# A convolution's taps move from a shared SBUF sum to PSUM, and a key/value product becomes a split product

## Chip, cores and metric

One core of one Trainium2 chip (8 cores, of which the program uses core 0). The metric is device time in microseconds (us) of one execution, the median of a few runs. Engines: TensorE (PE; PEld is its weight load), VectorE (DVE), ScalarE (ACT), GpSimd (POOL), SyncE (SP, which issues the DMAs here).

## What is computed

The program is a four-layer stack over 512 positions of width 1024, in fp32. Two hybrid layers (retention, dilated attention, gating, feed-forward) come first, then two layers of a second block. The second block's last layer begins with the convolution module, which the change is about, followed by cross attention to a memory of 256 positions and a gated feed-forward:

```python
def conv_module(xn, w_in, b_in, dw_w, dw_b, ln_g, ln_b, w_out):
    h = xn @ w_in + b_in
    a, gate = jnp.split(h, 2, axis=-1)
    h = a * jax.nn.sigmoid(gate)
    h = lax.conv_general_dilated(          # depthwise, causal, 31 taps
        h, dw_w[:, None, :], window_strides=(1,), padding=[(CONV_WIDTH - 1, 0)],
        dimension_numbers=('NWC', 'WIO', 'NWC'), feature_group_count=D_CONV) + dw_b
    h = jax.nn.silu(layernorm(h, ln_g, ln_b))
    return h @ w_out

def cross_attn(hn, memn, wq, wk, wv, q_gain, k_gain, wo):
    ...
    k = rmsnorm((memn @ wk).reshape(bsz, m_len, C_HEADS, C_HEAD_DIM), k_gain)
    v = (memn @ wv).reshape(bsz, m_len, C_HEADS, C_HEAD_DIM)
    ...
```

## The kernel before

**Products.** Nearly every matrix product is a split product: each fp32 operand is held as a high part (fp32r) and the low rest, and `mm3` (L325 to L328) issues three matmuls, high x high, high x low, low x high. Weights arrive by DMA from SP into `raw`; ScalarE casts the high part (L239) and VectorE, or GpSimd where `W.low` says so, subtracts it for the low part (L240), into one of eight slots `hl`. A few products are plain fp32 matmuls on the raw weights (L437) with no split; the keys and values of the last layer's memory are among them (`PLAIN_KV`).

**Order.** The order of instructions on each engine is fixed when the program is built. A modelled clock `X` runs a list of steps (a duration and a function that issues instructions); `X.at` puts a function at a modelled time, `X.drain` issues what is still due. Weights come in the order of `_weight_tiles`. An engine executes its instructions in that order, and waits at the head of its queue.

**The convolution** (`conv`) keeps channels on partitions: eight groups g of 128 channels by 512 positions. `prod` makes group g's two halves, value and gate, in two PSUM banks; `evac` (L1446 to L1448) turns them into `hp[:, g]`, with 30 zero columns ahead, by a tanh and an identity on ScalarE and one scalar-tensor-tensor on VectorE. Then 31 taps per group have to be summed into `y[:, g]` (SBUF):

- Groups 0 to 5: 18 taps on VectorE and 13 on GpSimd (`NPOOL`). A VectorE tap is one instruction, `y = hp * w + y` (L1520), with `w` a per-partition scalar. A GpSimd tap is a ScalarE product `m = hp * w` (L1510, three buffers) and a GpSimd add `y = y + m` (L1511). Both engines sum into the same `y[:, g]`, one after the other: in half of the groups GpSimd has the first phase, in the others VectorE.
- Groups 6 and 7: 14 taps on TensorE, as matmuls with diagonal weight matrices (L1559; VectorE makes the diagonals, L1552), copied by ScalarE to `y` (L1566), and 17 taps on VectorE (L1562), those of group 7 by halves of the sequence, with the second half put off (`late`).

A planner (`feed`, `choose`, `tap`) hands out taps from one queue per engine while PE steps run, by modelled costs (`T_TAP`, `T_SPLIT`, `T_SAME`: a tap that follows a tap into the same sum is counted 0.12 us dearer).

**The memory.** While this goes on, the layer's memory is normalised (L993), transposed and multiplied by the key and value weights in 16 steps of `memory_kv`, of four plain matmuls each: 10 of them before the means (`KV_LN`), 2 inside the first normalisation, and 4 inside the output product.

**After the taps.** The layer norm over channels is done per half of the sequence, 256 positions each: means by a ones matmul on PE (L1582), `spread` (L1611 on VectorE, a square on ScalarE, L1612), `total` (L1619, small variance matmuls), a reciprocal root and `across` (L1629), then per group `scale` (L1633 on VectorE, silu and cast on ScalarE, L1634 and L1635) and `apply` (low part). The output product takes four blocks t of 128 positions, each over eight weight tiles k and two banks; t 0 and 1 need the first half of the sequence, t 2 and 3 the second. The normalisation of the second half is put 14 modelled us (`AT_B`) after the first, so that it falls behind block 1, and the four remaining key/value steps stand ahead of block 2 (`before`). Six of the output weight tiles are held ahead (`AHEAD`), split in turn by GpSimd and VectorE (`LOW`).

## Time and profile before

| | |
|---|---|
| median of 3 runs | 2893.55 us (2886.67 to 2895.28) |
| profiled execution | 2889.6 us, span 2887.8 us, mean granted PE clock 0.983 |
| PE | 2758.8 us busy, 96% |
| PEld | 2289.5 us, 79% |
| DVE | 1341.2 us, 46% |
| ACT | 995.6 us, 34% |
| POOL | 484.3 us, 17% |

The profile is of one execution. Busy shares are averages over the whole span; the convolution, from about 2.09 to 2.39 ms, is a stage of its own in which they are different. Where a view speaks of a tap, the names are `y<-hp,conv_w,y`: the output, then the inputs (`conv_w` is the tile behind the pointer scalar `w`). `b` is any PSUM bank. Ends of matmuls are modelled, and fp32 matmuls have two records for one matmul of the program, so that counts on the rows of L437, L1559, L1582 and L1619 stand for half as many.

### The profile page before, as it was taken

Reading aid. Unit: us, or ns where it says so; the run is one execution under the profiler, and the core shown is the slowest. Engines: PE = TensorE matmul, PEld = TensorE weight load, DVE = VectorE, ACT = ScalarE, POOL = GpSimd, SP = SyncE. Lnnn points to the kernel's source line nnn. Section 1 sums busy time; section 2 is a strip of 40 time slices with the busy share of each in tenths; the row PEclk is TensorE's granted clock in tenths of the full one; section 3 lists DMA queues with packets and bytes.
Section 4 is the critical chain, followed back from the end, with each engine's and each line's share of the span. In section 5 each row is a group of like instructions: output and inputs, shape, how many; then the busy total and the mean of one; then the engine's idle time right before and its main releaser. Section 6 shows DMA issues by size and latency. Waiting matters only on the chain.

```text
span 2887.8 us, 34096 instructions
## 1 busy us (share of the span) xinstructions
PE 2758.8 (96%) x13624; PEld 2289.5 (79%) x13624; DVE 1341.2 (46%) x1952; ACT 995.6 (34%) x1737; POOL 484.3 (17%) x480
## 2 busy tenths in 40 slices
PE   7999999999999999999999999999995799999999
PEld 7888888879788888887678888888873368888887
DVE  4565222444464223355965442233499944432232
ACT  3434222333434223244454432223353235322231
POOL 3231000022130000023441300000076503100000
PEclk9999999999999999999999999999997899999999
DMA  4222322323213223222232213233231113132231
GB/s 149 76 72 76 114 95 88 124 62 103 69 60 102 96 94 117 91 78 81 78 116 74 94 54 107 90 105 114 83 106 51 66 44 103 52 103 97 93 117 51
DMA packets 76192, 255.95 MB, mean 89 GB/s; under 512 B 10369, under 2 KB 11777, under 8 KB 76033
## 3 DMA queue, kind: packets, MB, share of 16 engines
q1 hardware_dynamic: 76032, 253.77, 26.8%
q8 instruction: 107, 1.75, 0.2%
q14 instruction: 53, 0.43, 0.0%
HBM read 251.64 MB, written 2.10 MB: 88 GB/s over the span
## 4 chain that ended last, share of the span: by engine, by line
PE 82%; DVE 11%; ACT 3%; POOL 2%; issue 2%; DMA 0%; POOLq 0%; ACTq 0%; SPq 0%; DVEq 0%
PE b L326 25%; PE b L327 25%; PE b L328 25%; DVE y L1520 3%; PE b L348 1%; DVE y L1562 1%; DVE hl L240 1%; PE b L1402 1%; PE b L437 1%; DVE mask L1180 1%; ACT hl L239 1%; PE b L723 1%; DVE mask L1185 0%; POOL y L1511 0%; PE b L758 0%
## 5 line engine op out<-in xcount | busy, mean ns | idle before, releaser
L326 PE MATMUL b<-xh,hl 128*128 128x512 f32 (+1 forms) x1728 | 641.4, 371 | 1.6 <-ACT xh L336 1.6
L327 PE MATMUL b<-xl,hl 128*128 128x512 f32 (+1 forms) x1728 | 639.9, 370 | 1.7 <-DVE xl L337 1.7
L328 PE MATMUL b<-xh,hl 128*128 128x512 f32 (+1 forms) x1728 | 639.3, 370 | 0.0
L240 DVE TENSOR_TENSOR hl<-raw,hl 128x1024 fp32r<-128x1024 f32 (+1 forms) x398 | 471.8, 1210 | 149.6 <-ACT hl L239 146.2
L239 ACT CAST hl<-raw 128x1024 fp32r<-128x1024 f32 (+1 forms) x452 | 448.1, 1014 | 101.8 <-PE b L328 64.3
L326 PE MATMUL b<-hl,xh 128*128 128x512 f32 (+2 forms) x1088 | 412.8, 379 | 3.8 <-ACT xh L1635 1.7
L328 PE MATMUL b<-hl,xl 128*128 128x512 f32 (+2 forms) x1088 | 399.4, 367 | 3.2 <-DVE xl L337 3.0
L327 PE MATMUL b<-hl,xh 128*128 128x512 f32 (+2 forms) x1088 | 399.0, 367 | 2.5 <-DVE hl L240 2.4
L517 DVE TENSOR_TENSOR hraw<-sg,b 128x512 f32<-128x512 f32 (+1 forms) x96 | 61.8, 643 | 675.2 <-PE b L328 664.0
L326 PEld LDWEIGHTS b<-xh,hl 128*128 128x128 f32 x1728 | 326.4, 189 | 58.3 <-ACT xh L336 2.8
L327 PEld LDWEIGHTS b<-xl,hl 128*128 128x128 f32 x1728 | 326.4, 189 | 57.4 <-DVE xl L337 2.7
L328 PEld LDWEIGHTS b<-xh,hl 128*128 128x128 f32 x1728 | 326.2, 189 | 55.2
L516 ACT ACTIVATE sg<-b 128x512 f32<-128x512 f32 (+1 forms) x96 | 54.1, 563 | 675.2 <-PE b L328 675.2
L326 PE MATMUL b<-hl,hh 128*128 128x512 f32 x704 | 274.4, 390 | 0.0
L328 PE MATMUL b<-hl,hlw 128*128 128x512 f32 x704 | 273.9, 389 | 0.0
L327 PE MATMUL b<-hl,hh 128*128 128x512 f32 x704 | 273.9, 389 | 0.0
L326 PEld LDWEIGHTS b<-hl,xh 128*128 128x128 f32 x1088 | 208.2, 191 | 30.9 <-issue 5.7
L328 PEld LDWEIGHTS b<-hl,xl 128*128 128x128 f32 x1088 | 207.5, 191 | 27.2 <-DVE xl L337 4.4
L327 PEld LDWEIGHTS b<-hl,xh 128*128 128x128 f32 x1088 | 208.3, 191 | 23.4 <-DVE hl L240 3.7
L337 DVE TENSOR_TENSOR hlw<-hraw,hh 128x512 fp32r<-128x512 f32 x88 | 60.5, 691 | 210.5 <-ACT hh L336 210.5
L328 PEld LDWEIGHTS b<-hl,hlw 128*128 128x128 f32 x704 | 132.1, 188 | 27.5
L327 PEld LDWEIGHTS b<-hl,hh 128*128 128x128 f32 x704 | 132.2, 188 | 27.2
(276 smaller groups left out, 3132.5 us busy)
## 6 DMA issues: line engine op xcount, KB each, us to landing
raw<-in_ws SPq DMA_DIRECT2D x400, 512.0 KB, 3.5
raw<-in_ws SPq DMA_DIRECT2D x64, 384.0 KB, 3.1
x<-in_x SPq DMA_DIRECT2D x4, 512.0 KB, 6.4
mem<-in_mem SPq DMA_DIRECT2D x4, 512.0 KB, 5.4
out<-x SPq DMA_DIRECT2D x4, 512.0 KB, 2.6
raw<-in_ws SPq DMA_DIRECT2D x4, 336.0 KB, 2.8
gain<-in_g_mix_pre SPq DMA_DIRECT2D x2, 512.0 KB, 5.7
gain<-in_g_mix_post SPq DMA_DIRECT2D x2, 512.0 KB, 4.6
```

Of the source, the lines that this page charges most:

```text
L239: self.nc.scalar.copy(t[:, 0, :w], r[:, :w])
L240: self.low.tensor_sub(t[:, 1, :w], r[:, :w], t[:, 0, :w].bitcast(F32))
L326: PE.matmul(o, lh, rh, start=first, stop=False)
L327: PE.matmul(o, lh, rl, start=False, stop=False)
L328: PE.matmul(o, ll, rh, start=False, stop=last)
L337: (low or V).tensor_sub(dl, src, dh.bitcast(F32))
L348: PE.transpose(b[:, kk * P:(kk + 1) * P], xn[:, k * P:(k + 1) * P], ident)
L437: PE.matmul(b[:, :n], src[0][:, k, cols(t)], wh[:, kk], start=k == 0, stop=k == KD - 1)
L516: S.activation(sg[:, c0:c1], gb[:, c0:c1], AF.Silu)
L517: V.tensor_mul(hraw[:, n, c0:c1], sg[:, c0:c1], ub[:, c0:c1])
L723: PE.matmul(s[hh][:, :n], qkT["aq"][rs, pr, cols(t)], qkT["ak"][rs, pr, :n], start=True, stop=True)
L1520: V.scalar_tensor_tensor(o, i, w, o, op0=OP.mult, op1=OP.add)
```

## The change

VectorE no longer sums into `y`. Each group gets a PSUM bank `acc[g]`; VectorE's taps read `hp` and the bank and write the bank (`dve_tap`), GpSimd's sum stays in `y` (SBUF) and holds the bias, and one VectorE instruction per group adds the bank to `y` (`join`). For groups 6 and 7 the 14 diagonal matmuls start the sum in the same bank. GpSimd has 11 taps of 31 in groups 0 to 5 and now 6 in groups 6 and 7; VectorE has 20 and 11. With two sums no phase follows another, and the group products use banks 0 to 3 instead of 0 to 5, since banks 4 to 7 hold sums. ScalarE makes the diagonal matrices, 28 activations of 128 x 128, where VectorE made eight instructions.

The last layer's memory is split like everything else: its 16 weight tiles are cast and subtracted, and each key/value step is 12 matmuls instead of 4. 13 steps stand before the means, with group 7's diagonals ahead of the 13th, 3 stand inside the first half's normalisation, none in the output product. Weight order: the key/value tiles, then the output's, and none held ahead. The late half of group 7 goes; the second half's normalisation is issued right behind the first.

```diff
-PLAIN_KV = (1,)
-NPOOL = (13,) * 6
+NPOOL = (11,) * 6 + (6, 6)
-KV_LN = 10
-KV_OUT = 12
-AT_B = 14.0
-AT_PE = (1, 5)
-T_TAP = (0.72, 1.35)
+KV_LN = 13
+AT_PE = 12
+T_TAP = (0.78, 1.35)
...
-        out = by_rows(a["conv_w_out_2"][0]) if l else iter(())
-        for _ in range(AHEAD if l else 0):
-            yield next(out)
-        for i, w in enumerate((wk[:, :512], wk[:, 512:], wv[:, :512], wv[:, 512:])):
-            for t in moving(w):
-                yield t, l in PLAIN_KV
-                yield from itertools.islice(out, 1)
+        for w in (wk[:, :512], wk[:, 512:], wv[:, :512], wv[:, 512:]):
+            yield from moving(w)
+        if l:
+            yield from by_rows(a["conv_w_out_2"][0])
...
-            if l in PLAIN_KV:
-                mem["h"], mem["l"] = pl.tile([P, KD, 256], F32, tag="iq", name="mem"), None
+            if l:
+                mem["h"], mem["l"] = xh[:, :, 256:512], xl[:, :, 256:512]
...
+        where = {g: 4 + g % 2 for g in range(KD - 2)} | {KD - 2: 7, KD - 1: 6}
...
+        def pool_tap(g, j, first):
+            if first:
+                G.tensor_scalar(y[:, g, :], hp[:, g, j:j + T], dw[:, g, j:j + 1], db[:, g:g + 1], op0=OP.mult, op1=OP.add)
+            else:
+                m = pl.tile([P, T], F32, tag="m", name="m", bufs=4)
+                S.activation(m, hp[:, g, j:j + T], AF.Copy, scale=dw[:, g, j:j + 1])
+                G.tensor_add(y[:, g, :], y[:, g, :], m)
+
+        def dve_tap(g, j, first):
+            i, w = hp[:, g, j:j + T], dw[:, g, j:j + 1]
+            if first:
+                acc[g] = bank(where[g])
+                V.tensor_scalar(acc[g], i, w, None, op0=OP.mult)
+            else:
+                V.scalar_tensor_tensor(acc[g], i, w, acc[g], op0=OP.mult, op1=OP.add)
+
+        def join(g):
+            V.tensor_add(y[:, g, :], y[:, g, :], acc.pop(g))
+            joined.add(g)
+            ready.extend(((0, g), (1, g)))
...
-            def dve_tap(j, first, last):
-                o, i, w = y[:, g, :], hp[:, g, j:j + T], dw[:, g, j:j + 1]
...
-                    V.scalar_tensor_tensor(o, i, w, o, op0=OP.mult, op1=OP.add)
...
         def diagonals(g):
             st["dg", g] = d = []
-            for i, tag in enumerate(("s", "s", "s", "th")):
-                d.append(pl.tile([P, 4, P], F32, tag=tag, name="dg", bufs=3 if tag == "s" else 1))
-                V.tensor_tensor(d[i], ident[:, None, :].to_broadcast([P, 4, P]),
-                                dw[:, g, 4 * i:4 * i + 4, None].to_broadcast([P, 4, P]), op=OP.mult)
+            for i in range((NPE + 3) // 4):
+                d.append(pl.tile([P, 4, P], F32, tag="dg", name="dg", bufs=4))
+                for j in range(4 * i, min(4 * i + 4, NPE)):
+                    S.activation(d[i][:, j - 4 * i], ident, AF.Copy, scale=dw[:, g, j:j + 1])
...
-                        st[g] = [bank(2 * (g % 3)), bank(2 * (g % 3) + 1)]
+                        st[g] = [bank(2 * (g % 2)), bank(2 * (g % 2) + 1)]
...
-        X.drain()
+        means()
         means(True)
-        norm_half(0, 0.0, kv_steps[KV_LN:KV_OUT])
+        W.low = G
+        norm_half(0, 0.45, kv_steps[KV_LN:])
         X.drain()
         W.low = V
-        rest(1000)
-        X.at(AT_B, lambda: means(True))
-        X.at(AT_B, lambda: norm_half(1, 0.0))
+        norm_half(1, 0.55)
...
-            if t == 2 and k == 0:
-                X.run(kv_steps[KV_OUT:])
```

**How the order moves.** In the rows below, `b_` and a number is one PSUM bank in one use, and a count behind a row means the same instruction again. VectorE, the end of the taps in front of the means before:

```order
L1520 SCALAR_TENSOR_TENSOR y<-hp,conv_w,y 128x512 x20
L240 TENSOR_TENSOR hl<-raw,hl 128x1024
L1520 SCALAR_TENSOR_TENSOR y<-hp,conv_w,y 128x512 x4
L1562 SCALAR_TENSOR_TENSOR y<-hp,conv_w,y 128x512 x9
L1014 SCALAR_TENSOR_TENSOR kn<-b_16281,sm,g_15643 128x256 x2
L1014 SCALAR_TENSOR_TENSOR kn<-b_16282,sm,g_15643 128x256 x2
L1552 TENSOR_TENSOR dg<-ident,conv_w 128x512 x4
L1562 SCALAR_TENSOR_TENSOR y<-hp,conv_w,y 128x512 x5
```

and of the change (`b_16524`, `b_16310` and `b_16737` are the sums of three groups; L1588 is the subtraction of the mean, L1611 before):

```order
L229 TENSOR_TENSOR hl<-raw,hl 128x1024 x3
L1511 SCALAR_TENSOR_TENSOR b_16524<-hp,conv_w,b_16524 128x512 x3
L1514 TENSOR_TENSOR y<-y,b_16524 128x512
L1511 SCALAR_TENSOR_TENSOR b_16310<-hp,conv_w,b_16310 128x512 x8
L1514 TENSOR_TENSOR y<-y,b_16310 128x512
L1511 SCALAR_TENSOR_TENSOR b_16737<-hp,conv_w,b_16737 128x512 x11
L1514 TENSOR_TENSOR y<-y,b_16737 128x512
L1588 TENSOR_TENSOR y<-y,b_16823 128x256 x8
```

The taps read and write a bank, a join ends each group, weight splits (L240, now L229) stand among the taps up to the end, and the diagonals are gone from VectorE.

PE, from the first half's normalisation into the output product (L326 to L328, after it L315 to L317, are one split product). Before, where the product starts, and where the second half's normalisation stands (a row block t later):

```order
L1629 MATMUL b_16719<-ident,sm 128x128 x2
L326 MATMUL b_16775<-hl,xh 128x512
L327 MATMUL b_16775<-hl,xh 128x512
L328 MATMUL b_16775<-hl,xl 128x512
...
L328 MATMUL b_16829<-hl,xl 128x512
L1582 MATMUL b_16304<-y,ones 128x256
L1619 MATMUL b_16849<-ones,s 128x2 x16
L1629 MATMUL b_16895<-ident,sm 128x128 x2
L326 MATMUL b_16828<-hl,xh 128x512
```

and of the change:

```order
L1596 MATMUL b_16841<-ones,s 128x2 x8
L1606 MATMUL b_16923<-ident,sm 128x128 x2
L315 MATMUL b_16992<-hl,xh 128x512
L316 MATMUL b_16992<-hl,xh 128x512
L317 MATMUL b_16992<-hl,xl 128x512
L315 MATMUL b_16993<-hl,xh 128x512
L316 MATMUL b_16993<-hl,xh 128x512
L317 MATMUL b_16993<-hl,xl 128x512
L1596 MATMUL b_16988<-ones,s 128x2 x2
L315 MATMUL b_16992<-hl,xh 128x512
```

The second half's variance matmuls (`b_16988`) stand behind the first six matmuls of the output product, in pairs between its following blocks, and no longer all together behind one of its row blocks.

ScalarE at the same place (L1634 and L1635 are the silu and the cast of `scale`, L1612 the squares of the second half, L1030 a copy of values). Before:

```order
L1634 ACTIVATE s<-y,conv_ln_b,conv_ln_g 128x256
L1635 CAST xh<-s 128x256
L1030 COPY vt<-b_16613 128x512
L1030 COPY vt<-b_16614 128x512
L1612 ACTIVATE s<-y 128x256 x8
```

and of the change (L1611, L1612 and L1589 are the silu, the cast and the squares; L228 the cast of a weight; five more silu and cast pairs stand where the dots are):

```order
L1611 ACTIVATE s<-y,conv_ln_b,conv_ln_g 128x256
L1612 CAST xh<-s 128x256
L228 CAST hl<-raw 128x1024 x2
L1611 ACTIVATE s<-y,conv_ln_b,conv_ln_g 128x256
L1612 CAST xh<-s 128x256
L228 CAST hl<-raw 128x1024
...
L1611 ACTIVATE s<-y,conv_ln_b,conv_ln_g 128x256
L1612 CAST xh<-s 128x256
L228 CAST hl<-raw 128x1024
L1589 ACTIVATE s<-y 128x256 x8
```

The weight casts of the output product now stand among the first half's silu and cast pairs, and the squares of the second half behind all of them.

## Rows read from the trace of the kernel before

**Rows 1.** The page, the span in 40 equal slices of 72.2 us: tenths of VectorE's busy time, and the granted clock of PE in tenths.

```profile
DVE  4565222444464223355965442233499944432232
PEclk9999999999999999999999999999997899999999
```

**Rows 2.** Windows of the convolution: its taps up to the last tap of the first half, and a stretch inside it. Columns: the window, its length, busy us (and instructions) of PE, PEld, DVE, ACT and POOL, granted clock, DMA share, GB/s.

```profile
2097.80:2302.90 205.10, 154.54 (x508) 97.76 (x506) 199.10 (x182) 83.77 (x137) 144.54 (x91) 0.87 0.22 74
2196.00:2219.00 23.00, 6.11 (x11) 2.62 (x10) 22.96 (x15) 10.45 (x15) 22.14 (x14) 0.65 0.14 51
```

**Rows 3.** The chain of waits from the last tap to the output product's first matmul, and at its end the first matmul of the next stage: start and length in us, engine, output, line.

```profile
2303.01 0.71 PE b L1582 x2
...
2306.34 5.06 PE b L437 x8
...
2313.53 3.54 PE b L437 x8
...
2319.00 0.50 PE b L326
...
2389.84 0.47 PE b L326
```

**Rows 4.** Groups of VectorE instructions between 2085 and 2360 us, kept apart by shape: line, engine, operation, out<-in, sizes, count | busy us, mean ns of one | idle us just before them and what ended most of it.

```profile
L1520 DVE SCALAR_TENSOR_TENSOR y<-hp,conv_w,y 128x512 f32<-128x512 f32 x105 | 122.6, 1209 | 2.1 <-POOL y L1511 1.2
L1562 DVE SCALAR_TENSOR_TENSOR y<-hp,conv_w,y 128x512 f32<-128x512 f32 x17 | 24.7, 1455 | 0.4
L1562 DVE SCALAR_TENSOR_TENSOR y<-hp,conv_w,y 128x256 f32<-128x256 f32 x34 | 16.4, 482 | 0.7
L1448 DVE SCALAR_TENSOR_TENSOR hp<-th,av 128x512 f32<-128x512 f32 x6 | 7.4, 1226 | 0.0
L993 DVE SCALAR_TENSOR_TENSOR mem<-mem,sm,gain 128x1024 f32<-128x1024 f32 x2 | 4.5, 2309 | 0.0
L1014 DVE SCALAR_TENSOR_TENSOR kn<-b,sm,g 128x256 f32<-128x256 f32 x8 | 3.3, 476 | 0.0
```

**Rows 5.** Timeline of VectorE and GpSimd inside the taps: start and length in us of a run of like instructions, engine, line, count, and in brackets the idle time ahead of it. The first two stretches have no GpSimd instruction beside them; the last two lie beside each other.

```profile
2098.38 2.33 DVE L1520 SCALAR_TENSOR_TENSOR y<-hp,conv_w,y 128x512 f32<-128x512 f32 x3
2192.34 3.39 DVE L1520 SCALAR_TENSOR_TENSOR y<-hp,conv_w,y 128x512 f32<-128x512 f32 x5
2270.08 1.75 DVE L1520 SCALAR_TENSOR_TENSOR y<-hp,conv_w,y 128x512 f32<-128x512 f32 x1
2261.19 21.81 POOL L1511 TENSOR_TENSOR y<-y,m 128x512 f32<-128x512 f32 x13 [4.72 <-ACT m L1510]
```

**Rows 6.** GpSimd's adds: count, and the shortest, median and longest of them in ns.

```profile
L1511 POOL TENSOR_TENSOR y<-y,m x75: 1286/1597/5591, 2103.2 to 2281.4; 128x512 f32<-128x512 f32 x75
```

**Rows 7.** Timeline of VectorE and GpSimd in an earlier stage, the sparse layer: instructions that read a bank (`b`) and one that does not, beside a weight split on GpSimd.

```profile
1423.48 1.12 DVE L1164 SCALAR_TENSOR_TENSOR k<-b,sm,akn 128x128 f32<-128x128 f32 x4
1424.63 1.41 DVE L1098 TENSOR_TENSOR rot<-k,qcos 128x128 f32<-128x128 f32 x1
1423.50 2.39 POOL L240 TENSOR_TENSOR hl<-raw,hl 128x1024 fp32r<-128x1024 f32 x1 [0.53 <-ACT hl L239]
```

**Rows 8.** VectorE instructions of 128 x 512 with one source in a bank (residual adds, `x<-x,b`), and with all of them in SBUF and GpSimd at rest (`ypool<-s,ypool`): shortest, median and longest in ns, and when.

```profile
L394 DVE TENSOR_TENSOR x<-x,b x48: 678/687/689, 1540.2 to 2883.6; 128x512 f32<-128x512 f32 x48
L1258 DVE SCALAR_TENSOR_TENSOR ypool<-s,ypool x4: 692/692/693, 1332.9 to 1376.9; 128x512 f32<-128x512 f32 x4
```

**Rows 9.** Timeline of VectorE: a weight split beside GpSimd's adds, and one without.

```profile
2167.67 2.31 DVE L240 TENSOR_TENSOR hl<-raw,hl 128x1024 fp32r<-128x1024 f32 x1
2191.21 1.21 DVE L240 TENSOR_TENSOR hl<-raw,hl 128x1024 fp32r<-128x1024 f32 x1
```

**Rows 10.** Timeline of PE: the 14 diagonal matmuls of one group (two records each), then the output product with the second half's means, variances and root inside, and with its plain key/value steps (one in the first L437 row, three in the second); and two starts, three matmuls apart.

```profile
2219.03 14.71 PE L1559 MATMUL b<-hp,dg 128*128 128x512 f32 x28 [16.92 <-DVE dg L1552]
...
2334.12 0.60 PE L1582 MATMUL b<-y,ones 128*128 128x256 f32 x2
2335.68 3.73 PE L1619 MATMUL b<-ones,s 128*128 128x2 f32 x32 [0.96 <-ACT s L1612]
2340.78 0.69 PE L1629 MATMUL b<-ident,sm 128*128 128x128 f32 x2 [1.37 <-POOL sm L333]
2341.12 0.78 PE L326 MATMUL b<-hl,xh 128*128 128x512 f32 x1
...
2350.73 3.60 PE L437 MATMUL b<-raw,mem 128*128 128x512 f32 x8
2355.03 10.46 PE L437 MATMUL b<-raw,mem 128*128 128x512 f32 x24
...
2375.88 0.39 PE L326 MATMUL b<-hl,xh 128*128 128x512 f32 x1
...
2376.56 0.39 PE L326 MATMUL b<-hl,xh 128*128 128x512 f32 x1
```

**Rows 11.** Timeline of ScalarE at the first half's normalisation: two squares, the first silu and the last cast; and, over the whole span, the casts of weights with the shortest, median and longest in ns.

```profile
2311.82 0.86 ACT L1612 ACTIVATE s<-y 128x256 f32<-128x256 f32 x2 [4.89 <-PE b L1619]
2317.91 0.60 ACT L1634 ACTIVATE s<-y,conv_ln_b,conv_ln_g 128x256 f32<-128x256 f32 x1 [5.22 <-DVE y L1633]
...
2325.14 0.41 ACT L1635 CAST xh<-s 128x256 fp32r<-128x256 f32 x1
...
L239 ACT CAST hl<-raw x452: 757/1047/1095, 8.1 to 2840.4; 128x1024 fp32r<-128x1024 f32 x129, 128x768 fp32r<-128x768 f32 x21, 128x672 fp32r<-128x672 f32 x1
```

More of the change, by code (lines that the diff above doesn't have):

```diff
@@ L1 @@
 import heapq
-import itertools
 import math
@@ L1042, in lazy @@
         def lazy(i, mk):
-            steps.append(((16 if l in PLAIN_KV else 12) * 0.215, lambda: mk()[i][1]()))
+            steps.append((12 * 0.215, lambda: mk()[i][1]()))
         for n in range(4):
@@ L1452, in conv @@
         busy = {0: 0.0, 1: 0.0, "split": W.splits}
-        ends, begin, at = {}, {}, {"last": None}
+        ends, begin, at, acc = {}, {}, {"last": None}, {}
+        where = {g: 4 + g % 2 for g in range(KD - 2)} | {KD - 2: 7, KD - 1: 6}
         def start(e, item):
-            g, phase = item[:2]
-            return max(busy[e], X.now, ends.get(g, 1e9) if phase else begin[g])
+            g, kind = item[:2]
+            return max(busy[e], X.now, ends.get(g, 1e9) if kind else begin[g])
         def tap(e, i=0):
             q = queue[e]
-            g, phase, n, f = q[i]
-            if phase:
-                while any(it[0] == g and not it[1] for it in queue[1 - e]):
-                    tap(1 - e, next(i for i, it in enumerate(queue[1 - e]) if it[0] == g))
+            g, kind, n, f = q[i]
+            if kind:
+                while any(it[0] == g for it in gq):
+                    tap(1, next(i for i, it in enumerate(gq) if it[0] == g))
             q.pop(i)
             f()
-            busy[e] = start(e, (g, phase)) + T_TAP[e] * n + (T_SAME if not e and at["last"] == g else 0.0)
+            busy[e] = start(e, (g, kind)) + T_TAP[e] * n + (T_SAME if not e and at["last"] == g else 0.0)
             if not e:
                 at["last"] = g
-            if not phase and not any(it[0] == g and not it[1] for it in q):
+            elif not any(it[0] == g for it in q):
                 ends[g] = busy[e]
@@ L1478, in choose @@
                 if it[0] not in seen:
+                    if any(where[it[0]] == where[g] for g in seen):
+                        break
                     seen.add(it[0])
@@ new lines, in join, with rest @@
+        def join(g):
+            V.tensor_add(y[:, g, :], y[:, g, :], acc.pop(g))
+            joined.add(g)
+            ready.extend(((0, g), (1, g)))
+        def taps(g):
+            n = NPOOL[g]
+            begin[g] = X.now + 3.0
+            gq.extend((g, 0, 1, lambda j=j: pool_tap(g, j, j == TAPS - n)) for j in range(TAPS - n, TAPS))
+            if g < KD - 2:
+                rest(g, 0)
+        def rest(g, j0):
+            vq.extend((g, 0, 1, lambda j=j: dve_tap(g, j, j == 0)) for j in range(j0, TAPS - NPOOL[g]))
+            vq.append((g, 1, 1, lambda: join(g)))
@@ L1575, in conv, with by_diagonals @@
-        ready, late = [], []
+            for i in range((NPE + 3) // 4):
+                d.append(pl.tile([P, 4, P], F32, tag="dg", name="dg", bufs=4))
+                for j in range(4 * i, min(4 * i + 4, NPE)):
+                    S.activation(d[i][:, j - 4 * i], ident, AF.Copy, scale=dw[:, g, j:j + 1])
+        def by_diagonals(g, j0, j1):
+            d = st["dg", g]
+            if j0 == 0:
+                acc[g] = bank(where[g])
+            for j in range(j0, j1):
+                PE.matmul(acc[g], d[j // 4][:, j % 4], hp[:, g, j:j + T], start=j == 0, stop=j == NPE - 1)
+            if j1 == NPE:
+                begin[g] = X.now + (j1 - j0) * 0.86 + 0.5
+                rest(g, NPE)
@@ L1577, in means @@
+        ready, joined = [], set()
         def means(all_=False):
             for half, g in list(ready) if all_ else st.pop("ready", []):
-                if g == 0:
+                if not {KD - 4, KD - 3} <= joined:
+                    break
+                if ("mu", half) not in st:
                     st["mu", half] = bank(4 + half)
-                PE.matmul(st["mu", half][:, 0:256], ones, y[:, g, HALF[half]], start=g == 0, stop=g == KD - 1)
+                n = st["n", half] = st.get(("n", half), 0) + 1
+                PE.matmul(st["mu", half][:, 0:256], ones, y[:, g, HALF[half]], start=n == 1, stop=n == KD)
@@ L1639, in apply @@
             V.tensor_sub(xl[:, g, h], st.pop(("w", g)), xh[:, g, h].bitcast(F32))
-        def rest(n):
-            for _ in range(min(n, len(late))):
-                late.pop(0)[3]()
         def norm_half(half, step, fill=()):
@@ L1676, in conv, with beside, diagonal_steps @@
         steps += [prod(g, j, 0, 512, True, True) for g in range(2, KD) for j in range(2)]
[L1677 to L1690 removed]
+        steps.insert(-1, (0, lambda: diagonals(KD - 2)))
+        def beside(us, f):
+            steps.append((us, lambda: (means(), feed(us), f())))
+        def diagonal_steps(g, between=()):
+            cut = [NPE * i // 4 for i in range(5)]
+            for i in range(4):
+                if between:
+                    beside(0.5, between[i])
+                beside(0.86 * (cut[i + 1] - cut[i]), lambda i=i: by_diagonals(g, cut[i], cut[i + 1]))
+        diagonal_steps(KD - 2, [lambda t=t, h=h: kv["turn", t]((h,)) for t in range(2) for h in range(2)])
+        for i, (us, f) in enumerate(kv_steps[:KV_LN]):
+            if i == AT_PE - 4:
+                steps.append((0, lambda: diagonals(KD - 1)))
+            if i == AT_PE:
+                steps.append((0, lambda: X.until(turned_k)))
+                diagonal_steps(KD - 1)
+            beside(us, f)
         X.at(20.0, lambda: gain("next", a["norm_cross_2"][1], "g0"))
```

103 lines of the change are left out of this document (16 added, 87 removed).

## The prediction, made before the run

> **What bounds the kernel now.** I read the page's slices first, then the windows over the dip they show, then the chain of waits, then VectorE's and GpSimd's groups and timelines. In the slices VectorE (DVE) stands at 9 tenths in four neighbouring slices around 2.2 ms while TensorE's (PE's) clock falls to 7 and 8 [rows 1]: that is the convolution, and nowhere else does DVE fill a slice. The windows give it limits. From the first tap at 2097.8 to the last tap of the first half of the sequence at 2302.9, DVE is busy 199.1 of 205.1 us and PE's records cover 154.5; in 2196 to 2219 PE works 6.1 of 23.0 us and its granted clock is 0.65, towards the lower of its two levels [rows 2]. So this stretch is DVE's. The chain then leaves DVE at 2303.0, passes two means, two key/value steps and the normalisation of the first half, and reaches the output product at 2319.0 [rows 3]; that product ends at 2389.6, just ahead of the next stage's first matmul at 2389.84 [rows 3]. After 2303 it is a chain of hand-overs; before it, it is DVE's sum of durations.
>
> Why is DVE full? Its taps cost 122.6, 24.7 and 16.4 us, 163.7 in all, for 105 + 17 + 17 whole taps (34 are halves) [rows 4]: 1.18 us each. Alone, three taps into the same sum take 2.33 us (0.78 each) and five that alternate between two sums 3.39 (0.68 each). Beside GpSimd (POOL) one takes 1.75, and POOL's 13 adds in the same stretch 21.81, so 1.68 each: the two engines take turns [rows 5]. POOL's own add takes 1.29 at best and 1.60 in the median [rows 6].
>
> **What makes them take turns** decides this change, because after it a tap reads one SBUF tensor (hp) and the bank. An earlier stage shows a near relative: a scalar-tensor-tensor that reads a bank, an SBUF tensor and a pointer scalar. Four of them, begun at 1423.48, took 1.12 us together inside a POOL split that ran from 1423.50 to 1425.89; the next DVE instruction has two SBUF tensors, is no larger, and took 1.41, ending just behind that split [rows 7]. Bank readers pass, readers of two SBUF tensors wait. So I count the taps as free of POOL.
>
> **The change, DVE up to the last join.** The number of DVE taps stays: 6 x 20 + 2 x 11 = 142, against 6 x 18 + 2 x 17. In the new order 116 follow another sum or another instruction and 26 follow their own sum; the last 11 do so in one row (first order piece). No row shows DVE writing a bank. I take 0.70 and 0.80, the rows' 0.68 and 0.78 plus a small allowance: 81.2 + 20.8 = 102.0 us. Bounds: 0.68 and 0.78 below (-2.9), and above, the planner's own new constants 0.78 and 0.90, which are no measurement (+11.9).
>
> [...]
>
> Beside the taps, DVE has up to the last join: 26 weight splits (16 of them now for keys and values and four for the output). A split reads two SBUF tensors, so it still meets POOL: 2.31 beside it, 1.21 without [rows 9]. POOL is seldom idle, but a split will arrive anywhere within an add of 1.29 and wait half of it on average: 1.21 + 0.64 = 1.85, x 26 = 48.1 (bounds 1.21 and 2.31: -16.6, +12.0). Six gates at 1.23 and a half one, 7.8; two memory scalings at 2.31, 4.6; eight key scalings, 3.3 [rows 4]; four memory splits from a bank and eight joins, priced as an add from a bank at 0.69 [rows 8], 2.7 and 5.5; one gain 0.5. The diagonal matrices go to ScalarE, 28 small activations within an engine that worked 83.8 of the 205.1 us [rows 2]. Sum 102.0 + 72.5 = 174.5. I leave DVE the 6.0 us of idle time that it has now. The last join ends at 2097.8 + 174.5 + 6.0 = 2278.3 where the last tap ended at 2303.0: **-24.7**.
>
> Would another engine end later? POOL: 78 taps at 1.29 are 101, plus some 35 DVE instructions that hold it for about 0.9 each, plus 10 for small work: 142, from 2102 to 2244. PE: the split keys and values start when DVE has made the last memory split, by my running sum at 2193, then 13 steps of 12 matmuls at 0.68 per three [rows 10], 2.73 a step, with 14 diagonal matmuls ahead of the 13th, 14.7 in one batch now [rows 10]: 2243, about 2250 with its transposes. Both are ahead of 2278, so the key/value product's own gain (a plain step takes 3.60 [rows 10]) is worth nothing there.
>
> **From the last join to the output product** 16.0 us now, with two plain steps of 5.06 and 3.54 inside [rows 3]. After: three split steps, 8.2 at full clock, the first of them slower since PE will have waited; one more pair of means. I take 17.0: **+1.0**.
>
> **The output product** takes 70.6 us now, 2319.0 to 2389.6. Four plain steps stand in it, 3.60 and 10.46 by the modelled ends of their matmuls and about 0.16 less each by the pitch to the next matmul, so 13.7 [rows 10]; they go, hidden above: **-13.7**. The second half's normalisation interrupts PE once now, from 2334.12 to 2341.12, 7.0 us [rows 10]. The change moves that forward: the variance matmuls of the second half stand on PE behind the first row block of the product (second order piece), and their squares stand on ScalarE behind all of the first half's work (third piece). There eight silu/cast pairs of 0.94, from 2317.91 to 2325.54 [rows 11], and four casts of weights at 1.05 [rows 11] make 11.8 us, the first pair 1.1 ahead of the product; with a square of 0.43 (two in 0.86 [rows 11]) PE gets its first variance operand 11.1 after the product's start and has 1.4 of work before it: a wait of 9.7, then variance matmuls, of whose 3.73 [rows 10] I count half, 1.9, since the squares run ahead of them, and 1.7 from the last of them to the next matmul (1.37 of waiting and the spread of the root [rows 10]). 13.3 in place of 7.0: **+6.3**. What this new wait holds up is the product's other 31 blocks, and nothing else.
>
> **Sum:** -24.7 + 1.0 - 13.7 + 6.3 = -31.1. It is made against the profiled execution, 2889.6 us (span 2887.8); the median of the three runs, 2893.55, is 3.95 above it. Taken from the median: 2862.
>
> **Rivals.** (1) The time goes into a coupling instead. ScalarE makes POOL's products and the casts of the splits in one queue, and it already waits for POOL's adds. If casts arrive late, DVE waits at the head of its queue and every tap behind it too. For it: 13 more splits before the joins, almost all of them beside POOL. Against it: DVE idles only 6.0 of 205.1 us today [rows 2]. With every split at the 2.31 of rows 9 (+12.0) and DVE idle for another 5, the gain is 14: 2879.
>
> (2) Slower: taps on a bank are dear. Each is read, added and written back there, and no row shows the write. The 31.1 us are spread over 150 accesses, so the change decides at +0.21 us, a tap of 0.91. If the tap costs the 1.18 it costs today, without POOL, the sum is +0.48 x 142 = 68 us later, 37 slower than now: 2930. Against it: nothing separates bank and SBUF reads in rows 8; the diff's planner counts 0.78.
>
> (3) The change does not do what it says: hp or the pointer scalar still meets POOL. Then taps stay at 1.18 and the 13 extra splits at 2.31 come on top: about 2935. Against it stand the four instructions of rows 7.
>
> **How the numbers follow.** Forecast 0.71, rival 1 0.17, rival 2 0.09, rival 3 0.03. The forecast's own lower end: taps at the rows' price (-2.9), half of the splits meeting no POOL (-8), no idle DVE (-6), the second half's wait as short as now (-6), a faster restart (-3): 2836. Its upper end: the planner's constants (+11.9) and six more on the splits: 2880. Range 2836 to 2886, which takes in most of rival 1 and leaves out rivals 2 and 3. A measurement of this kernel tells about 0.3%, 8.7 us, from no change: faster means below 2884.9. Forecast and two thirds of rival 1 are faster, the rest of rival 1 is the same: 0.82, 0.06, 0.12 slower.
>
> **What would show each step.** Taps near 0.70 with POOL adds at 1.3 beside them, splits still stretched; last join near 2278; no key/value step inside the output product; a PE wait of some 10 us behind that product's first block, released by ScalarE's squares. I am wrong if taps into a bank take over 0.9 us, if DVE waits for casts for more than 15 us, or if PE, not DVE, is last at the means.

## The result and the profile after

The changed kernel takes 2860.05 us (median of 4 runs, 2853.04 to 2861.09), the one before 2894.41 in the same comparison: a ratio of 0.9882, 95% interval 0.9858 to 0.9905. A second series on another occasion, beside the experiments below, gave 2855.54 against 2893.67, 0.9878 (0.9859 to 0.9896). The profiled execution of the change has a span of 2859.3 us against 2887.8.

**Slices.** They read as [rows 1] do; the page of after:

```profile
DVE  4565222444464323344974443223389744422232
PEclk9999999999999999999999999999999889999999
```

In the convolution (slices 30 to 32) VectorE reads 8, 9 and 7 where it read 9, 9 and 9, and the clock has no 7 any more. The 9 further left, at 1.37 ms, is the sparse layer's, before and after.

**Windows**, the columns of [rows 2]: from the first VectorE tap to the end of the last join; from there to the output product; the output product.

```profile
2102.20:2276.70 174.50, 146.53 (x582) 108.20 (x580) 159.41 (x199) 96.21 (x170) 120.49 (x89) 0.92 0.28 95
...
2276.70:2296.00 19.30, 16.93 (x74) 13.54 (x74) 3.65 (x12) 4.35 (x11) 0.93 (x2) 0.77 0.00 1
2296.00:2360.50 64.50, 52.92 (x240) 43.76 (x241) 30.81 (x56) 33.02 (x60) 15.70 (x13) 0.86 0.19 57
```

VectorE now idles 15.1 of 174.5 us ahead of the last join, where it idled 6.0 of 205.1.

**VectorE's groups** between 2085 and 2360 us, as in [rows 4], and the shortest, median and longest of the taps and of GpSimd's adds, as in [rows 6]:

```profile
L1511 DVE SCALAR_TENSOR_TENSOR b<-hp,conv_w,b 128x512 f32<-128x512 f32 x136 | 94.9, 746 | 0.9
L229 DVE TENSOR_TENSOR hl<-raw,hl 128x1024 fp32r<-128x1024 f32 x33 | 49.6, 1511 | 14.2 <-ACT hl L228 14.0
...
L1441 DVE SCALAR_TENSOR_TENSOR hp<-th,av 128x512 f32<-128x512 f32 x6 | 7.0, 1162 | 1.8 <-ACT av L1440 1.8
...
L1514 DVE TENSOR_TENSOR y<-y,b 128x512 f32<-128x512 f32 x8 | 5.4, 679 | 0.2
```

```profile
L1511 DVE SCALAR_TENSOR_TENSOR b<-hp,conv_w,b x136: 734/745/757, 2103.0 to 2275.2; 128x512 f32<-128x512 f32 x136
L1503 POOL TENSOR_TENSOR y<-y,m x70: 1262/1295/3352, 2101.6 to 2234.5; 128x512 f32<-128x512 f32 x70
...
L229 DVE TENSOR_TENSOR hl<-raw,hl x30: 1204/1226/2318, 2088.3 to 2256.2; 128x1024 fp32r<-128x1024 f32 x30
```

The longest of 136 taps is 23 ns above the shortest, with GpSimd working 120 us beside them. GpSimd's median add is now near its shortest. Gates and splits, which read two SBUF tensors, are still stretched, but not all of them: the longest split took 2.32 us, and more than half of the 30 took 1.23 or less, about what one takes alone (1.21 [rows 9]).

**Timeline** of the two, as in [rows 5]: seven taps into one bank, five that alternate between two, and the adds beside either.

```profile
2103.01 5.51 DVE L1511 SCALAR_TENSOR_TENSOR b<-hp,conv_w,b 128x512 f32<-128x512 f32 x7
...
2172.26 3.38 DVE L1511 SCALAR_TENSOR_TENSOR b<-hp,conv_w,b 128x512 f32<-128x512 f32 x5
...
2101.60 15.18 POOL L1503 TENSOR_TENSOR y<-y,m 128x512 f32<-128x512 f32 x10 [0.36 <-ACT m L1502]
...
2160.57 15.59 POOL L1503 TENSOR_TENSOR y<-y,m 128x512 f32<-128x512 f32 x10
```

0.79 a tap in one sum and 0.68 when sums alternate, beside adds: what SBUF sums took with GpSimd at rest [rows 5].

**The way to the product and through it**: the chain, as in [rows 3], then PE's timeline, as in [rows 10].

```profile
2276.01 0.70 DVE y L1514
2276.75 1.24 PE b L1559 x2
...
2279.95 0.64 PE b L315
...
2294.47 0.70 PE b L1606 x2
2295.26 0.43 DVE y L1610
2295.78 0.61 ACT s L1611
...
2308.77 0.33 ACT s L1589
2309.14 1.01 PE b L1596 x4
...
2360.61 0.70 DVE x L383
```

```profile
2258.78 0.60 PE L1559 MATMUL b<-y,ones 128*128 128x256 f32 x2
...
2276.75 2.08 PE L1559 MATMUL b<-y,ones 128*128 128x256 f32 x4 [8.24 <-DVE y L1514]
...
2294.47 0.69 PE L1606 MATMUL b<-ident,sm 128*128 128x128 f32 x2 [1.37 <-POOL sm L322]
2296.87 0.79 PE L315 MATMUL b<-hl,xh 128*128 128x512 f32 x1 [1.71 <-ACT xh L1612]
...
2309.14 1.01 PE L1596 MATMUL b<-ones,s 128*128 128x2 f32 x4 [9.34 <-ACT s L1589]
```

PE has its 13 key/value steps done at 2258.8, starts on the means there and waits 8.24 us for the last join, so VectorE is last; then 20.2 us pass to the product's first matmul; and behind the product's first block PE waits 9.34 us for the second half's squares.

**The stage.** Executions of the same code differ in when they reach the convolution, so the stage is measured from its first VectorE instruction (`hb`) to the pair of residual adds that ends it (the start of the last pair before the next stage).

```profile
2075.65 0.17 DVE L1433 TENSOR_SCALAR hb<-conv_b 128x8 f32<-128x8 f32 x1
...
2389.01 1.37 DVE L394 TENSOR_TENSOR x<-x,b 128x512 f32<-128x512 f32 x2 [1.74 <-PE b L328]
```

```profile
2079.86 0.16 DVE L1426 TENSOR_SCALAR hb<-conv_b 128x8 f32<-128x8 f32 x1
...
2360.61 1.37 DVE L383 TENSOR_TENSOR x<-x,b 128x512 f32<-128x512 f32 x2 [1.67 <-PE b L317]
```

The first fence is before, the second after: 313.4 and 280.8 us. What follows the stage is 498.8 and 498.7 us. So the change took 32.6 us from this stage, and the profiled execution gave 4.2 back ahead of it.

### The profile page after: what moved, and what is told of

It reads as the page before. It is cut to its first block, busy times and chain, and to the rows that moved or that the text cites. A ratio compares the mean times of both kernels' runs of the same rounds, so it can differ in the third digit from the quotient of the medians.

```text
span 2859.3 us, 34280 instructions
## 1 busy us (share of the span) xinstructions
PE 2744.4 (96%) x13688; PEld 2302.1 (81%) x13688; DVE 1294.8 (45%) x1952; ACT 1012.5 (35%) x1774; POOL 472.9 (17%) x483
## 4 chain that ended last, share of the span: by engine, by line
PE 83%; DVE 7%; POOL 4%; ACT 4%; issue 2%; DMA 0%; POOLq 0%; ACTq 0%; DVEq 0%; SPq 0%
PE b L315 26%; PE b L317 25%; PE b L316 25%; POOL y L1503 2%; DVE b L1511 1%; PE b L337 1%; PE b L1395 1%; ACT hl L228 1%; DVE hl L229 1%; DVE mask L1173 1%; POOL sm L322 1%; PE b L712 1%; DVE mask L1178 0%; PE b L733 0%; PE b L747 0%
## 5 line engine op out<-in xcount | busy, mean ns | idle before, releaser
L315 PE MATMUL b<-xh,hl 128*128 128x512 f32 (+1 forms) x1728 | 641.9, 371 | 1.6 <-ACT xh L325 1.6
L317 PE MATMUL b<-xh,hl 128*128 128x512 f32 (+1 forms) x1728 | 640.2, 370 | 0.0
L229 DVE TENSOR_TENSOR hl<-raw,hl 128x1024 fp32r<-128x1024 f32 (+1 forms) x411 | 489.5, 1215 | 157.6 <-ACT hl L228 154.5
L228 ACT CAST hl<-raw 128x1024 fp32r<-128x1024 f32 (+1 forms) x468 | 464.5, 1016 | 102.3 <-PE b L317 65.5
L315 PE MATMUL b<-hl,xh 128*128 128x512 f32 (+2 forms) x1152 | 442.4, 384 | 3.4 <-ACT xh L1612 1.7
L317 PE MATMUL b<-hl,xl 128*128 128x512 f32 (+2 forms) x1152 | 425.8, 370 | 4.5 <-DVE xl L326 4.3
L316 PE MATMUL b<-hl,xh 128*128 128x512 f32 (+2 forms) x1152 | 425.6, 369 | 1.8 <-DVE hl L229 1.8
L315 PEld LDWEIGHTS b<-xh,hl 128*128 128x128 f32 x1728 | 326.8, 189 | 58.6 <-ACT xh L325 2.8
L317 PEld LDWEIGHTS b<-xh,hl 128*128 128x128 f32 x1728 | 326.6, 189 | 55.4
L315 PE MATMUL b<-hl,hh 128*128 128x512 f32 x704 | 274.5, 390 | 0.0
L317 PE MATMUL b<-hl,hlw 128*128 128x512 f32 x704 | 274.0, 389 | 0.0
L315 PEld LDWEIGHTS b<-hl,xh 128*128 128x128 f32 x1152 | 221.4, 192 | 34.0 <-issue 8.3
L317 PEld LDWEIGHTS b<-hl,xl 128*128 128x128 f32 x1152 | 220.6, 191 | 31.4 <-DVE xl L326 5.7
L316 PEld LDWEIGHTS b<-hl,xh 128*128 128x128 f32 x1152 | 221.6, 192 | 25.6 <-DVE hl L229 3.1
L326 DVE TENSOR_TENSOR hlw<-hraw,hh 128x512 fp32r<-128x512 f32 x88 | 60.5, 691 | 210.5 <-ACT hh L325 210.5
L317 PEld LDWEIGHTS b<-hl,hlw 128*128 128x128 f32 x704 | 132.2, 188 | 27.5
```

The lines of the kernel that those rows point to most:

```text
L228: self.nc.scalar.copy(t[:, 0, :w], r[:, :w])
L229: self.low.tensor_sub(t[:, 1, :w], r[:, :w], t[:, 0, :w].bitcast(F32))
L315: PE.matmul(o, lh, rh, start=first, stop=False)
L316: PE.matmul(o, lh, rl, start=False, stop=False)
L317: PE.matmul(o, ll, rh, start=False, stop=last)
L326: (low or V).tensor_sub(dl, src, dh.bitcast(F32))
```

## Experiments

All but the first row are the changed kernel or edits of it. "Stage" is the length just described, from each run's one profile. e0_after and the profile above (second row) are the same code and differ by 1.4 us in it, so less than that can't be read from one profile.

| run | time, us (range) | stage, us | last join after `hb`, us |
|---|---|---|---|
| before | 2893.67 (2886.63 to 2897.78) | 313.4 | - |
| the change, as above | 2860.05 (2853.04 to 2861.09) | 280.8 | 196.8 |
| e0_after | 2855.54 (2854.14 to 2858.24) | 279.3 | 196.1 |
| e1_sbuf_sum | 2898.33 (2896.65 to 2902.38) | 321.7 | 238.0 |
| e2_plain_kv | 2858.51 (2857.19 to 2859.39) | 279.8 | 197.6 |
| e3_pool13 | 2850.58 (2850.32 to 2852.39) | 274.8 | 191.1 |
| e4_late_half | 2853.04 (2845.88 to 2854.68) | 274.3 | 196.2 |
| e5_no_pool | 2840.09 (one run) | 260.3 | 176.2 |
| e6_sbuf_no_pool | 2838.05 (one run) | 261.2 | 176.2 |
| e7_kv16 | 2850.75 (2843.32 to 2853.45) | 273.3 | 196.0 |
| e8_kv16_late | 2847.38 (2841.98 to 2849.44; a fourth run took 13672.55 and is not counted) | 267.7 | 194.9 |
| e9_all | 2843.02 (2837.26 to 2844.69) | 262.2 | 190.4 |
| e10_sources | 2884.28 (one run) | 303.7 | 218.1 |

**e0_after.** No edit. 

> The changed kernel once more, as it is, on the chip of the runs beside it, so that differences of a few us can be read: 2860 (2853 to 2865).

 It came out at the lower end of that.

**e1_sbuf_sum.** The bank of groups 0 to 5 is taken back (for space, ScalarE's products `m` get three buffers instead of four):

```diff
-                acc[g] = bank(where[g])
+                acc[g] = pl.tile([P, T], F32, tag="acc", name="acc", bufs=2)
                 V.tensor_scalar(acc[g], i, w, None, op0=OP.mult)
```

> VectorE sums its taps of groups 0 to 5 in an SBUF tile of its own instead of a bank; two sums, the join and all the rest of the change stay (the products of ScalarE have three buffers, not four, for lack of space). Theory (VectorE's instructions with two SBUF sources take turns with GpSimd, those with one SBUF source and a bank don't): these 114 taps go from 0.75 to about 1.2 us in the mean, 1.6 to 1.8 beside an add, GpSimd's adds from 1.3 to 1.6 in the median, taps of groups 6 and 7 stay at 0.75; some 50 us more on VectorE, of which idle time takes up to 10: 2900 (2885 to 2925), slower than before the change or the same. Rival (what helped is that the two engines no longer wait for each other's phase in one sum, wherever it lies): taps stay at 0.75, 2860.

```profile
L1511 DVE SCALAR_TENSOR_TENSOR acc<-hp,conv_w,acc 128x512 f32<-128x512 f32 x114 | 130.0, 1189 | 0.3
...
L1511 DVE SCALAR_TENSOR_TENSOR b<-hp,conv_w,b 128x512 f32<-128x512 f32 x22 | 16.6, 754 | 0.6
...
L1511 DVE SCALAR_TENSOR_TENSOR b<-hp,conv_w,b x22: 745/756/756, 2285.7 to 2310.9; 128x512 f32<-128x512 f32 x22
...
L1503 POOL TENSOR_TENSOR y<-y,m x70: 1276/1622/3590, 2096.2 to 2270.8; 128x512 f32<-128x512 f32 x70
```

VectorE's groups of this run, then when the 22 bank taps and GpSimd's adds ran: the 114 taps that took 0.75 us on a bank take 1.19 in SBUF, and GpSimd's median add goes from 1.30 back to 1.62. (The 22 bank taps of this run started after GpSimd's last add, so they tell nothing here.) The whole gain of the stage is gone, and 8 us more; the time's ratio to before is 1.0021 (1.0011 to 1.0030). Two separate sums in SBUF do not make a tap cheaper: 1.19 against 1.21 in the shared sum [rows 4].

**e10_sources.** Of groups 0 to 5, the taps of even ones read two SBUF tensors and write a bank, those of odd ones read a bank and an SBUF tensor and write SBUF (again with three buffers of `m`):

```diff
...
-                acc[g] = bank(where[g])
-                V.tensor_scalar(acc[g], i, w, None, op0=OP.mult)
+                two = [pl.tile([P, T], F32, tag="acc", name="acc", bufs=2), bank(where[g])]
+                st["from", g], acc[g] = two if g % 2 == 0 else two[::-1]
+                V.tensor_scalar(st["from", g], i, w, None, op0=OP.mult)
...
-                V.scalar_tensor_tensor(acc[g], i, w, acc[g], op0=OP.mult, op1=OP.add)
+                V.scalar_tensor_tensor(acc[g], i, w, st["from", g], op0=OP.mult, op1=OP.add)
```

> Which side of a tap must be the bank for it to pass GpSimd. The changed kernel, but the taps of groups 0, 2 and 4 read hp and an SBUF tile and write a bank, those of groups 1, 3 and 5 read hp and a bank and write an SBUF tile (the running sum is given up for that: only the last tap of these groups is kept, so the convolution's output is not summed). Theory (two SBUF sources make an instruction take turns with GpSimd): the taps of even groups take 1.1 to 1.3 us in the mean and up to 1.8 beside an add, those of odd groups stay near 0.7. Rival (an SBUF destination does it): the other way round. Third (either is enough): both above 1.1.

```profile
L1514 DVE SCALAR_TENSOR_TENSOR b<-hp,conv_w,acc x57: 743/1124/1843, 2104.0 to 2268.9; 128x512 f32<-128x512 f32 x57
L1514 DVE SCALAR_TENSOR_TENSOR acc<-hp,conv_w,b x57: 730/735/748, 2120.0 to 2280.4; 128x512 f32<-128x512 f32 x57
```

Shortest, median and longest tap of each kind, in one run, all within one convolution: the sources decide, the destination does nothing. The three buffers of `m` are the same for both kinds, so they are not what stretched e1's taps.

**e5_no_pool and e6_sbuf_no_pool.** GpSimd's 70 adds left out, once with banks, once with SBUF sums.

```diff
-            gq.extend((g, 0, 1, lambda j=j: pool_tap(g, j, j == TAPS - n)) for j in range(TAPS - n, TAPS))
+            gq.append((g, 0, 1, lambda: pool_tap(g, TAPS - n, True)))
```

> The changed kernel with GpSimd's taps left out except the first of each group (70 adds and ScalarE's 70 products are gone, so 10 taps of 31, or 5, are missing from the sum). It shows what GpSimd's adds cost VectorE. Theory (taps on a bank don't meet GpSimd, instructions with two SBUF sources do): taps stay at 0.73 to 0.76 us, weight splits go from 1.5 to 1.21, gates from 1.16 to 0.69; VectorE's busy time from the first tap to the last join falls by 10 to 13 us from 159.4, and its waits for ScalarE's casts (8.8 us) shrink since ScalarE has 48 us less to do: last join 12 to 20 us earlier, 2840. Rival (the taps on a bank still pay GpSimd something): taps fall below 0.70 us, the join is more than 20 us earlier.

> The sums of groups 0 to 5 in an SBUF tile and GpSimd's 70 adds left out (10 taps of 31, or 5, are missing from the sum), to be set beside the run with sums in banks and the adds left out (2840.1 us, taps 0.747). Theory (SBUF and bank differ only through GpSimd): taps at 0.69 to 0.79, in the mean as the bank's to 0.02 us, time within 4 us of 2840. Rival (a bank is cheaper or dearer by itself): taps differ by more than 0.04 us, the time by 6 us or more.

The groups of e5, and the taps of e6:

```profile
L1511 DVE SCALAR_TENSOR_TENSOR b<-hp,conv_w,b 128x512 f32<-128x512 f32 x136 | 94.9, 747 | 0.9
L229 DVE TENSOR_TENSOR hl<-raw,hl 128x1024 fp32r<-128x1024 f32 x30 | 38.0, 1279 | 8.3 <-ACT hl L228 8.1
```

```profile
L1511 DVE SCALAR_TENSOR_TENSOR acc<-hp,conv_w,acc x114: 735/745/1101, 2099.3 to 2234.9; 128x512 f32<-128x512 f32 x114
```

Taps on banks change by a nanosecond when the adds go (means of 0.746 and 0.747); SBUF taps fall from a mean of 1.19 to 0.760, with a median of 0.745, the bank's own. Stages 260.3 and 261.2: without GpSimd's adds nothing separates bank from SBUF. The last join is 20.7 and 20.0 us earlier than in the change's two profiles, at the upper end of the 12 to 20 expected: splits are hardly stretched (1.28 in the mean, 1.54 in the change over the same window), and VectorE waits less for ScalarE, which also has 70 products less to make. That is what the remaining contention and GpSimd's share of ScalarE still cost this kernel, together.

**e2_plain_kv.** Memory, keys and values plain again (the steps are the plain matmuls of L437 before), output tiles held as before the change; `m` and the diagonals get fewer or shared buffers for space.

```diff
-                mem["h"], mem["l"] = xh[:, :, 256:512], xl[:, :, 256:512]
+                mem["h"], mem["l"] = pl.tile([P, KD, 256], F32, tag="iq", name="mem"), None
...
-                yield from moving(w)
+                for t in moving(w):
+                    yield t, bool(l)
+                    yield from itertools.islice(out, 1)
```

> The changed kernel with the last layer's memory, keys and values plain again (4 fp32 matmuls a step, no split of its 16 tiles, six output tiles held ahead and split in turn by GpSimd and VectorE, as before the change); the sums in banks stay, 13 steps before the means, 3 in the first normalisation, none in the output product. Theory (VectorE is still the bound up to the last join, so the split keys' gain on PE is worth nothing there and their splits cost VectorE): 16 splits at about 1.5 and four memory splits at 0.7 leave VectorE, 13 steps at 3.43 instead of 2.73 put 9 us on PE; last join some 10 us earlier than 2276.7, set by PE's diagonals of group 7: 2850 (2843 to 2857). Rival (PE is as close a bound as VectorE, and the split products give what the change gained there): last join 9 us or more later, 2869 (2863 to 2875).

```profile
2207.46 16.76 PE L430 MATMUL b<-raw,mem 128*128 128x512 f32 x32 [6.74 <-DMA raw<-in_ws]
```

```profile
2266.88 8.67 DVE L1515 SCALAR_TENSOR_TENSOR b<-hp,conv_w,b 128x512 f32<-128x512 f32 x11 [19.95 <-PE b L1548]
```

PE's and VectorE's timelines of this run. Neither number came: the stage is as long as the change's. VectorE, 16 splits lighter, was done early and then waited 19.95 us for group 7's diagonals on PE, which stood behind plain steps of 3.4 us and a 6.74 us wait for a raw tile. So the split keys move work from PE to VectorE at no gain and no loss here, and my theory that the last join would come 10 us earlier was wrong: with plain steps PE sets the last join (197.6 us after `hb`), about a microsecond from where VectorE sets it with split ones (196.1 and 196.8).

**e3_pool13.** `NPOOL = (13,) * 6 + (8, 8)`. 

> The changed kernel with 13 taps of groups 0 to 5 and 8 of groups 6 and 7 on GpSimd instead of 11 and 6: 16 taps leave VectorE. Theory (VectorE's queue sets the last join, GpSimd is done 40 us ahead of it): 16 x 0.70 = 11 us off VectorE, 16 x 1.37 = 22 us onto GpSimd, which is then done near 2257, ahead of the join; 12 us more on ScalarE make casts later, so 5 to 9 us of it remain: 2849 (2846 to 2853). Rival (ScalarE, which makes GpSimd's products and the casts, is the next bound): no gain, 2855 to 2860.

 The stage is 4.6 and 6.0 us shorter than the change's two profiles, the last join 5.4 us earlier than their mean: half of the 11 us that VectorE lost, as expected. The rest went into the splits and the waits for casts ahead of them. Over the same window, the change first and this run second, a split's mean in ns and then the idle time in us:

```profile
L229 DVE TENSOR_TENSOR hl<-raw,hl 128x1024 fp32r<-128x1024 f32 x30 | 45.9, 1539 | 12.3 <-ACT hl L228 12.2
...
L229 DVE TENSOR_TENSOR hl<-raw,hl 128x1024 fp32r<-128x1024 f32 x30 | 49.0, 1643 | 14.7 <-ACT hl L228 14.5
```

**e4_late_half.**

```diff
-        norm_half(1, 0.55)
+        X.at(14.0, lambda: norm_half(1, 0.0))
```

> The changed kernel with the second half's normalisation issued 14 modelled us later, as before the change, so that its squares and variance matmuls stand behind the output product's first row block or further. Theory (PE waits 9.3 us behind the product's first block because the squares stand on ScalarE behind the first half's silus and weight casts): the wait goes or shrinks to 1 or 2 us, the product takes about 57 instead of 63.7 us: 2853 (2849 to 2856). Rival (the product's first block waits for the silus themselves, so the wait only moves): 2860.

```profile
2287.13 0.79 PE L315 MATMUL b<-hl,xh 128*128 128x512 f32 x1 [1.71 <-ACT xh L1612]
...
2306.99 3.63 PE L1596 MATMUL b<-ones,s 128*128 128x2 f32 x32
2311.99 0.69 PE L1606 MATMUL b<-ident,sm 128*128 128x128 f32 x2 [1.37 <-POOL sm L322]
...
2345.38 1.27 DVE L383 TENSOR_TENSOR x<-x,b 128x512 f32<-128x512 f32 x2
```

PE's timeline, and the residual adds: the wait ahead of the variance matmuls is gone, 1.37 for the root stays. The product's length, from its first matmul to the last pair of residual adds, goes from 63.7 to 58.3 us. The median moved by less than that (2853.0 against 2855.5): the stage is where it can be seen.

**e7_kv16, e8_kv16_late, e9_all.** `KV_LN = 16`; that with e4's edit; both with e3's.

> The changed kernel with all 16 key/value steps ahead of the means, none inside the first half's normalisation. Theory (between the last join and the output product the three split steps lie on the path, 10 of the 20.2 us, while PE waits 8 us and more for VectorE just ahead of the last join): the way from the last join to the product's first matmul goes from 20.2 to 10 or 11 us, the last join moves by 0 to 2 us: 2848 (2845 to 2851). Rival (the path there is the normalisation's own chain, and the steps fill its gaps): 2 us or less, 2854 to 2856.

```profile
2275.65 1.83 PE L1559 MATMUL b<-y,ones 128*128 128x256 f32 x4 [3.08 <-DVE y L1514]
...
2288.35 0.80 PE L315 MATMUL b<-hl,xh 128*128 128x512 f32 x1 [1.71 <-ACT xh L1612]
```

PE's timeline of e7: from the last join (2275.6) to the product 12.8 us instead of 20.2, with the join in its place; 10 or 11 was expected. The three steps went into PE's waits, of which 3.08 us are left of 8.24 at the join.

> Both: all key/value steps ahead of the means, and the second half's normalisation 14 modelled us later. If the two costs are independent, their gains add: 9 and 6 us off the stage, 2841 (2837 to 2846). If the output product's start is bound by the splits of its weights in either case, the sum gives less than 10: 2847 or more.

> All three gains in one kernel: 16 key/value steps ahead of the means, the second half's normalisation 14 modelled us later, 13 and 8 taps on GpSimd. By the runs one by one the stage from the convolution's start to the last residual add was 280.7 us in the change, 273.3, 274.3 and 274.8 with one of them each, 267.7 with the first two. If all add: 262 us and 2839 (2834 to 2844). If with fewer taps on VectorE PE is the last at the means (16 key/value steps of 2.73 stand ahead of them), the third gain is lost: 266 to 268 us, 2845.

From the change's mean stage of 280.1 us, e3, e4 and e7 take 5.3, 5.8 and 6.8; the sum of the last two is 12.6 and e8 takes 12.4, the sum of all is 17.9 and e9 takes 17.9. The gains add, as far as single profiles 1.4 us apart can tell. e9_all is the fastest kernel here that sums all taps, 2843.02, a ratio of 0.9831 (0.9817 to 0.9845) to before. Its stage of 262.2 is the 262 expected; its time is 4 us above the 2839 expected, and e8's 6 above its 2841, outside the range given. For e8 the single gains had been taken as 9 and 6 us, and the two runs show 6.8 and 5.8.

```profile
2268.36 1.03 PE L1559 MATMUL b<-y,ones 128*128 128x256 f32 x4
```

In e9 PE starts its last means without a wait, 3.5 us after the last join (2264.9): it is now PE that is last there, which was the condition of the rival, and yet the third gain was not lost.

## Why the prediction was right

The forecast was 2862 from a sum of -31.1; measured were 2860.05, 2855.54 and -32.6 in the stage. The mechanism held; that the sum came so near is luck in part, since its terms missed both ways: up to the last join -30.7 in place of -24.7, from there to the product +4.2 in place of +1.0, in the product -6.3 in place of -7.4. By its steps:

- **Taps free of GpSimd**: shown. No tap is stretched (734 to 757 ns), e1 gives the gain back when the bank is taken away (1.19 us a tap), e10 shows that it is the sources: 1124 ns in the median and up to 1843 with two SBUF inputs, 735 and at most 748 with one. The earlier stage's four instructions [rows 7] were the right relative. 142 taps took 99.4 us (94.9, and 4.5 for the six that open a sum) for the 102.0 I counted; records of neighbouring instructions overlap a little (the five alternating taps of the timeline above start 0.66 us apart), and counted from start to start they took 96.9.
- **A bank's own price**: no run shows one. Medians of 735 ns (bank as source, e10) and 745 (bank as source and destination, the change) stand beside 745 for SBUF alone in e6.
- **VectorE's other work** was over-counted, its idle time under-counted: 60.0 us in place of 72.5 (62.5 counted from start to start), mostly because the 26 splits took 40.9 us and not 48.1, and 15.1 us of idle time in place of 6.0, of which 8.8 are waits for ScalarE's casts (rival 1's wait came, its dearer splits did not). That splits wait for half an add each was not so: more than half took no longer than alone, and the longest 2.32. First tap to last join: 174.5 for 180.5. That the clock time of the last join, 2276.7, is so near the forecast 2278.3 is partly luck, since this execution reached its first tap 4.4 us later than the one before.
- **From the last join to the product** +1.0 was too little: 20.2 against 16.0, +4.2. I priced three steps at 8.2 and one more pair of means. The steps took 10.3: the first ran at the lower granted clock after PE's wait (0.52 from 2279.95 to 2283.6 with matmuls 0.43 apart, 1.00 from there to 2290 with 0.23). And the last variance matmuls, 1.69 us, now stand behind the last step, so that PE waits 1.37 for the root; before, the second plain step (2313.53 to 2317.07 [rows 3]) stood behind them and covered it, and PE went on without a wait. e7 shows what taking the steps out of the path gives back: 7.4 us. PE's line of before:

```profile
2316.90 0.38 PE L1629 MATMUL b<-ident,sm 128*128 128x128 f32 x2
```

- **Output product**: -7.4 was the sum of its two terms, 70.0 became 63.7, -6.3. e4, which issues the second half as late as before, tells them apart about: 70.0 to 58.3 is -11.7 where the key/value steps were put at -13.7, and 58.3 to 63.7 is +5.4 where the moved half was put at +6.3. The wait of 9.7 was 9.34, on ScalarE's squares, and e4 takes it away. Not counted was the granted clock, 0.86 over the product and 0.95 before: it read 0.50 from 2296 to 2313, around the wait, 0.91 to 2320 and 1.00 from there on.
- **The split products' own gain** I put at nothing up to the join, because PE would be done near 2250, 28 us ahead of VectorE. In the change it was done at 2258.8, 18 us ahead. e2 shows no net gain either, but for another reason than mine: the split steps do save PE time that VectorE would have to wait for (19.95 us in e2), and their 16 weight splits cost VectorE about as much, since the last joins lie within about a microsecond.
- **GpSimd's end**: the last add ended at 2235.8 where 2244 was counted. The 0.9 us for which some 35 VectorE instructions were to hold GpSimd, 31.5 in all, was my estimate and stands in no row; the 70 adds took 107.3 us, 19.0 more than 70 of the shortest (1262 ns).

Rival 2 (dear bank taps) and rival 3 (contention stays) fall by the taps' 734 to 757 ns. Rival 1 was there in part and did not decide.

Readings of mine that were wrong without moving the forecast: rows 1 show three neighbouring full slices in the convolution and the fourth in the sparse layer, not four in a row and none elsewhere; and the range's upper bound of 2886 lies 6 us above the 2880 that its own terms give.

What stays open: how much of e5's 20.7 us is contention on splits and gates, and how much ScalarE's time for GpSimd's products; no run took one away without the other.

## What to carry to other kernels

Where VectorE and GpSimd both work for long, look at what VectorE's instructions read: with one source in a bank they ran as fast beside GpSimd's adds as without them here (0.746 and 0.747 us a tap, the change and e5), with two in SBUF they were stretched (1.19 in e1, 0.760 without the adds in e6), and a running sum is easy to move. When an engine is relieved by 30 us, count what it will wait for next: here ScalarE's casts (8.8 us of waits in the change) and PE's diagonals (19.95 in e2) were close behind it. And compare stages from a mark inside the program, when the stages ahead of it can move by more than the effect.
